# One place for each use: raw weights and row sums in the feed-forward stage of a one-core encoder layer

## The chip, the core and the metric

The kernel runs on one core of a Trainium2 chip. A core has a matrix engine (PE, with its weight loader PEld), a vector engine (DVE), an activation engine (ACT), a general engine (POOL) and a synchronising engine (SP). Each takes its own instructions strictly in the order in which they were queued. Transfers between main memory and the core's own memory are issued from the queue of SP, ACT or POOL, so an issue that has to wait holds up what stands behind it on that engine. All issued transfers share 16 transfer engines.

The metric is the time of one execution in microseconds (us), and the median of several runs is quoted. Beside it stands one profiled execution, from which all rows come.

## What is computed

The reference is one layer of a streaming encoder on 512 tokens of width 1024: four parallel token mixers, a cross-attention, and a gated feed-forward part. The change touches the last of these:

```python
hf = _rms_norm(x, norm_ffn_pre[l])
u = _dwconv_causal(hf @ w_up[l], ffn_dw[l]) + ffn_dw_b[l]
u_g, u_v = jnp.split(u, 2, axis=-1)
yff = (jax.nn.silu(u_g) * u_v) @ w_down[l]
x = x + _rms_norm(yff, norm_ffn_post[l])
```

`w_up` is 1024 x 5632 and `w_down` is 2816 x 1024, so the hidden width of 2816 is 22 blocks of 128 channels. Everything is float32.

## The kernel before

**Products of float32.** Every operand is split in two parts, a rounded high part and the low rest (ACT writes the high part, DVE the low one: L201 and L202 for weights, L1646 and L1647 in the last stage). A product is then three matmuls, all recorded at L244. Split weights go to a ring of four places `wh` and four `wl`; a split must wait until PE has finished with the place four splits earlier.

**The up-projection** (`up_jobs`, L1662) runs over the 22 channel blocks, each with a gate part and a value part. Blocks of even number after the third are done plainly (`plain`, L1691): 8 steps of three 512-column matmuls for each part. Blocks 3, 5, ... 19 are done by `seven` (L1722): the gate and value weights of one block are taken as a 2 x 2 block matrix and multiplied by seven products in place of eight. That needs sums of weights, which POOL makes from the raw weights (L1732 to L1735): it writes the tile `sums` and overwrites parts of the raw tiles `z.g` and `z.v`. One period of the loop at the end of `up_jobs` is one `seven` block and the next plain block. On PE its order is: `a` (body_a, two products), the plain gate part, `b` (two products), the first half of the plain value part, `c`, `d` (one product each), the second half, and `e` (one product). For `b` the split reads `sums`, for `c` the raw tile `z.v`, and for `d` the second half of `z.g`. The next block's `z.g` and `z.v` are loaded on SP's queue (L1740, named `wq`) and `z.g` is split for the next `a`. A weight job is fetched three jobs ahead of its products.

**The sums for the last product.** The down-projection uses seven products too, over 11 pairs of blocks. What it needs of sums of `w_down` is made during the up-projection by `Sums` (L557): for pair q, `load` brings two tiles of 512 KB from `w_down` (L568, named `wp`, on ACT's queue), `add` does four additions of 128 x 512 on POOL (L572 to L575; on DVE for pair 0), and `store` writes both tiles to a buffer in main memory named `sums` (L579, on ACT's queue). The first stored tile is complete after the third addition, the second after the fourth.

**The down-projection** (`down_jobs`, L1827) goes over the 11 pairs twice (phase 0 and phase 1), two jobs for a pair, so 44 raw tiles (`dw`) are loaded on SP's queue from `w_down` and from the stored sums (L591), split by ACT and DVE (L1646, L1647) and multiplied. A job of phase 0 is 12 matmuls of 512 columns. `activations` (L1841) splits the hidden values of a pair; `down_sums` (L1654) has made sums of them on POOL (L1658 to L1660), and a further subtraction on POOL at L1862 prepares phase 1.

**Four places for three uses.** `wp`, `wq` and `dw` tiles, all 128 x 1024, share one tag `dw` with four places. A new tile gets whichever place comes free, and a tile that was named earlier in the program goes first.

**Order.** The order of instructions on each engine is set when the program is built, by a planner that follows the program on a model of the chip: an instruction is queued when the model has its inputs and its place ready. `issue_after(ins)` adds that whatever in the block is on the same engine as `ins` is queued behind it; it puts no condition on instructions of other engines.

Of the kernel before, what the change touches and what calls it, by code (L numbers as in the profile page):

```python
# [17 lines left out]
F32 = mybir.dt.float32  # L18
# [7 lines left out]
P = 128  # L26
# [60 lines left out]
def hybrid_layer(ctx: ExitStack, tc: tile.TileContext, a: dict, out: bass.AP):  # L87
# [1109 lines left out]
    def then(f):  # L1197

        return None, None, f
# [420 lines left out]
    def open_ffn():  # L1620
        bg.drain("n1")
        close(ns.work_)
        close(ns.xp_)
        close(ns.xm_)
        ns.fp_, ns.fp = new_pool("ffn", False)
        ns.work = ns.fp
        ns.quart = [ns.fp.tile([P, 4, S // 2], F32, tag=f"qa{q}", name="qa") for q in range(NF // 2)]
        ns.tok = [ns.fp.tile([P, 4, 4, S // 2], F32R, tag=n, name=n) for n in ("tokh", "tokl")]
        ns.post = ns.fp.tile([P, D], F32, name="g_ffn")
        G.dma_start(ns.post, a["norm_ffn_post"][0].partition_broadcast(P))  # L1630

    def token_sums():

# [28 lines left out]
    def up_jobs():  # L1662
# [19 lines left out]
        def add_sums(q, eng, anchor):  # L1682
            with tc.issue_after(st[anchor]):
                ns.sums.add(q, eng)
# [15 lines left out]
        for n in range(4):  # L1700
            def body(hi, lo, n=n):
                j, i = divmod(n, 2)
                if n == 0:
                    bg.drain("n0")
                ps = bank(("mm", "sc")[n % 2])
                if n == 3:
                    channel_major(ps, (hi, lo), ns.hf, first, lambda: bg.drain("n1"))
                else:
                    (channel_major if n else by_pass)(ps, (hi, lo), ns.hf, first)
                held.append((j, i, ps, (hi, lo)))  # L1710
                if n == 3:
                    open_ffn()
                    ns.sums = Sums(w_down, NF // 2, lambda: ns.fp.tile([P, D], F32, tag="dw", name="wp", bufs=4), A,
                                   "sums")
                    ns.sums.load(0)
                    token_sums()
                    for j, i, ps, w in held:
                        (channel_major if i or j else by_pass)(ps, w, ns.hf, second)
                        done(j, i, ps)
            yield *cols(w_up, n % 2 * DFF + n // 2 * P), body, V, same, HALF_SHIFT  # L1720

        def seven(j):  # L1722

            z = SimpleNamespace()

            def load_a():
                z.g, z.v = [load_block(j, i) for i in range(2)]
                w = split_weights(z.g, [P, NK, P], shift=HALF_SHIFT)
                z.s = ns.fp.tile([P, D], F32, tag="z7", name="sums2")
                a11, a12, a21, a22 = (x[:, c] for x in (z.g, z.v) for c in (slice(0, S), slice(S, D)))  # L1730
                s1, s2 = z.s[:, :S], z.s[:, S:]
                G.tensor_tensor(s1, a21, a22, ALU.add)  # L1732
                G.tensor_tensor(s2, s1, a11, ALU.subtract)
                G.tensor_tensor(a21, a11, a21, ALU.subtract)
                G.tensor_tensor(a12, a12, s2, ALU.subtract)  # L1735
                return w

            def load_block(j, i):
                raw = ns.fp.tile([P, D], F32, tag="dw", name="wq", bufs=4)
                SP.dma_start(raw.rearrange("p (k c) -> p k c", k=NK), block(j, i)[0])  # L1740
                return raw

            def product(ps, w, k0, x, start):
                for k in range(4):
                    mm3(ps, w[0][:, k0 + k], w[1][:, k0 + k], x[0](k), x[1](k), start and k == 0, k == 3, True)

            def part(k0, t):
                return [lambda k, h=h: h[:, k0 + k, (first, second)[t]] for h in ns.hf]

            def summed(i):  # L1750
                return [lambda k, h=h: h[:, i, k] for h in ns.tok]

            def body_a(*w):
                z.r1, z.r2 = bank("sc"), bank("tr")
                z.m = ns.fp.tile([P, 2, HALF], F32, tag="mu", name="mu")
                product(z.r2[:, first], w, 0, part(0, 0), True)
                A.copy(z.m[:, 0], z.r2[:, first])
                product(z.r1[:, first], w, 4, part(4, 0), True)
                V.tensor_tensor(z.r1[:, first], z.r1[:, first], z.m[:, 0], ALU.add)

            def body_b(*w):
                product(z.r2[:, first], w, 4, summed(1), False)
                A.copy(z.m[:, 1], z.r2[:, first])  # L1763
                product(z.r1[:, second], w, 0, summed(0), True)
                A.copy(z.m[:, 0], z.r1[:, second])

            def body_c(*w):
                z.w = w
                product(z.r2[:, first], w, 0, summed(2), False)
                V.tensor_tensor(z.r2[:, second], z.r2[:, first], z.m[:, 0], ALU.add)  # L1770

            def body_d(*w):
                product(z.r1[:, second], w, 0, part(4, 1), False)
                V.tensor_tensor(z.r1[:, second], z.r1[:, second], z.m[:, 1], ALU.add)
                done(j, 0, z.r1)

            def end():
                product(z.r2[:, first], z.w, 4, summed(3), False)
                done(j, 1, z.r2)

            return (load_a, body_a, (lambda: split_weights(z.s, [P, NK, P], shift=HALF_SHIFT), None, body_b),
                    (lambda: split_weights(z.v, [P, NK, P], shift=HALF_SHIFT), None, body_c),
                    (lambda: split_weights(z.g[:, S:], [P, 4, P], shift=HALF_SHIFT), None, body_d), then(end))

        for q, j in enumerate(range(3, NF - 2, 2)):
            load_a, body_a, b, c, d, e = seven(j)
            if q:
                a = load_a, None, body_a
            else:
                a, early = (lambda: (ns,), None, lambda *w: body_first(*early)), []  # L1790
                body_first = body_a
                yield then(lambda f=load_a: early.extend(f()))
                yield plain(2, 0)
                yield plain(2, 1, lambda: (add_sums(0, V, "taps"), sums_step("store", 0, "first")))
            tail = {}

            def first_half(hi, lo, tail=tail):
# [8 lines left out]
                done(j, 1, tail["ps"])  # L1806

            yield a
            yield then(lambda q=q: ns.sums.load(q + 1))
            yield plain(j + 1, 0)  # L1810
            yield b
            yield then(lambda q=q: ns.sums.add(q + 1, G))
            yield (*block(j + 1, 1), first_half)
            if j + 4 > NF:
                ns.pair_sums = []
                yield then(lambda: (down_places(("z7", 2)), down_sums(0, 1)))
            yield c
            yield d
            yield then(lambda q=q: ns.sums.store(q + 1))
            yield then(lambda j=j, f=second_half: f(j + 1))  # L1820
            yield e
        q = NF // 2 - 1
        yield then(lambda: (ns.sums.load(q), down_places(("tokh", 8), ("tokl", 1))))
        yield plain(NF - 1, 0, lambda: (ns.sums.add(q, G), down_sums(2, 3)))
        yield plain(NF - 1, 1, lambda: (ns.sums.store(q), down_sums(*range(4, NF // 2))))

    def down_jobs():  # L1827
        pairs, hold, half = NF // 2, 4, S
# [3 lines left out]
        def load(n):  # L1832
            while len(raws) < min(n, 2 * len(order)):
                (phase, q), job = order[len(raws) // 2], len(raws) % 2
                raw = ns.fp.tile([P, D], F32, tag="dw", name="dw", bufs=4)
                load_parts(raw, ns.sums.parts(phase, job, q))
                raws.append(raw)

# [2 lines left out]
        def activations(phase, q):  # L1841
# [14 lines left out]
            if phase:  # L1856
                split_to(hi, lo, x[:, 1:].rearrange("p a b -> p (a b)"))
            else:
                for i, part in enumerate((x[:, :2], ns.pair_sums[q])):
                    cut = slice(i * S, i * S + S)  # L1860
                    split_to(hi[:, cut], lo[:, cut], part.rearrange("p a b -> p (a b)"))
                G.tensor_tensor(x[:, 1], x[:, 2], x[:, 1], ALU.subtract)  # L1862
            form = dict(a=n, b=256)
            parts[phase, q] = hi.rearrange("p (a b) -> p a b", **form), lo.rearrange("p (a b) -> p a b", **form)

        def weights(phase, q, job):
# [10 lines left out]
                split_to(*both, raw[:, :half])  # L1877
                return [both],
            if (phase, q) == (1, pairs - 1):
                hi, lo = (ns.fp.tile([P, D], F32R, tag="dw", name="dwr", bufs=4) for _ in range(2))  # L1880
            else:
                hi, lo = weights_tile("wh")[:, :D], weights_tile("wl")[:, :D]
            split_to(hi, lo, raw)
# [66 lines left out]
        def ends():  # L1950
# [20 lines left out]
                            next(waiting)  # L1971
                return x

            spare = [ns.fp.tile([P, D], F32, tag="dw", name="o", bufs=4) for _ in range(2)]
            spare.append(gp.tile([P, WB], F32, tag="wr", name="wr", bufs=2)[:, :D])
            with tc.manual_schedule(engines={e.engine for e in (PE, V, A, G)}):
                for name, t, i, x in (("M4", 0, 0, z7), ("M4", 1, 0, z7), ("M2", 0, 0, m1), ("M3", 0, 1, u),
# [78 lines left out]
```

## Time and profile before

| | us |
|---|---|
| median of 3 runs | 1073.95 (1070.86 to 1075.01) |
| the profiled execution | 1072.34 |
| its span, first to last instruction | 1070.5 |
| PE busy in the span | 1034.7 (97%) |
| DVE / ACT / POOL busy | 858.4 / 536.9 / 308.6 |
| stretch 0 to 690 us: PE busy | 687.79 of 690.00 |
| stretch 690 to 945 us (up-projection): PE busy | 237.15 of 255.00 |
| stretch 945 to 1070.5 us (down-projection): PE busy | 109.71 of 125.50 |

Rows of the profile read as follows. A group or timeline row gives the line of the kernel, the engine, the operation, the output tile, an arrow, and the input tiles; in square brackets stands how long the engine was idle before it, and what ended the idle time. A row of waits gives who waited, for whom, the total in us, how often, and the longest. A row of stretches gives the stretch, its length, the busy time of each engine (with the count of instructions), the granted clock of PE, the share of transfer time, and GB/s. The chain of waits is followed back from the last instruction; its rows give the start, the duration and what it was. Matmuls are pipelined and recorded with more than their issue interval, so the interval between starts is PE's true pace.

### The profile page before, as it was taken

To read this page: it belongs to the slowest core of one execution; us is meant where nothing else is said; L and a number is where in the kernel's file an instruction comes from. 1 tells how busy PE (TensorE), PEld (TensorE's weight loads), DVE (VectorE), ACT (ScalarE), POOL (GpSimd) and SP (SyncE) were. 2 spreads that over 40 slices of the span, in tenths; PEclk is the share of its full clock that TensorE was granted. 3 is DMA by queue.
4 is the path that set the end of the run, shared out by engine and by line. 5 is a ranking of instruction groups with operands and counts; after the bars stand their busy time and mean duration, and the time that the engine had idled before them with its cause. 6 is when DMAs were issued, how large, how long until landed. Compare 5 with 4: busy or idle time off the path is not lost.

```text
span 1070.5 us, 15271 instructions
## 1 busy us (share of the span) xinstructions
PE 1034.7 (97%) x5513; PEld 889.1 (83%) x5513; DVE 858.4 (80%) x1283; ACT 536.9 (50%) x898; POOL 308.6 (29%) x319
## 2 busy tenths in 40 slices
PE   9999999999999999999999999998889989997997
PEld 7888888888889988888888999997878879875886
DVE  7899998678787668878679887877766867798796
ACT  5332222386655567657345656544443545544662
POOL 4001000100111144322010310392576555596001
PEclk9999999999999999999999999999989999999999
DMA  7954333334544357756469432344746655526762
GB/s 256 291 169 104 111 99 104 81 99 118 150 115 128 81 143 190 204 159 188 142 217 278 154 119 79 94 130 153 252 143 213 205 189 177 169 87 205 238 205 91
DMA packets 194129, 169.41 MB, mean 158 GB/s; under 512 B 25295, under 2 KB 165692, under 8 KB 194053
## 3 DMA queue, kind: packets, MB, share of 16 engines
q1 hardware_dynamic: 185011, 136.69, 43.0%
q10 hardware_dynamic: 6482, 23.21, 5.9%
q0 software_dynamic: 2560, 8.54, 2.6%
q8 instruction: 43, 0.70, 0.3%
q14 instruction: 33, 0.27, 0.1%
HBM read 142.18 MB, written 26.23 MB: 157 GB/s over the span
## 4 chain that ended last, share of the span: by engine, by line
PE 75%; POOL 12%; DMA 7%; issue 2%; DVE 2%; ACT 1%; ACTq 0%; POOLq 0%; SPq 0%; DVEq 0%
PE ps_mm L244 36%; PE ps_av L244 19%; PE ps_tr L244 10%; PE ps_sc L244 7%; DMA wq<-in_w_up 3%; POOL wp L573 2%; DMA sums<-wp 2%; POOL wp L572 2%; POOL wp L574 2%; DMA wp<-in_w_down 1%; PE ps_tr L250 1%; POOL wq L1735 1%; POOL sums L1732 1%; POOL qa L1660 1%; DVE wl L202 1%
## 5 line engine op out<-in xcount | busy, mean ns | idle before, releaser
L201 ACT CAST wh<-wr 128x1024 fp32r<-128x1024 f32 (+1 forms) x122 | 127.2, 1046 | 174.9 <-PE ps_mm L244 68.9
L202 DVE TENSOR_TENSOR wl<-wr,wh 128x1024 fp32r<-128x1024 f32 (+1 forms) x122 | 162.7, 1336 | 37.1 <-ACT wh L201 36.5
L244 PE MATMUL ps_mm<-hth,wh 128*128 128x512 f32 (+1 forms) x464 | 170.8, 376 | 4.4 <-ACT wh L201 4.0
L244 PE MATMUL ps_mm<-htl,wh 128*128 128x512 f32 (+1 forms) x464 | 170.7, 376 | 0.0
L244 PE MATMUL ps_mm<-hth,wl 128*128 128x512 f32 (+1 forms) x464 | 170.4, 376 | 0.0
L244 PEld LDWEIGHTS ps_mm<-hth,wh 128*128 128x128 f32 x464 | 85.8, 188 | 20.2 <-ACT wh L201 4.2
L244 PEld LDWEIGHTS ps_mm<-hth,wl 128*128 128x128 f32 x464 | 85.7, 188 | 15.5
L244 PEld LDWEIGHTS ps_mm<-htl,wh 128*128 128x128 f32 x464 | 85.6, 188 | 15.0
L244 PE MATMUL ps_av<-htl,wh 128*128 128x512 f32 (+1 forms) x256 | 95.1, 371 | 0.0
L244 PE MATMUL ps_av<-hth,wl 128*128 128x512 f32 (+1 forms) x256 | 95.0, 371 | 0.0
L244 PE MATMUL ps_av<-hth,wh 128*128 128x512 f32 (+1 forms) x256 | 95.0, 371 | 0.0
L697 DVE SCALAR_TENSOR_TENSOR y<-y,par,y 128x508 f32<-128x508 f32 (+29 forms) x120 | 82.8, 730 | 0.1
L244 PEld LDWEIGHTS ps_av<-hth,wl 128*128 128x128 f32 x256 | 48.5, 190 | 8.0
L244 PEld LDWEIGHTS ps_av<-htl,wh 128*128 128x128 f32 x256 | 48.4, 189 | 7.7
L244 PEld LDWEIGHTS ps_av<-hth,wh 128*128 128x128 f32 x256 | 48.5, 189 | 7.5
L1647 DVE TENSOR_TENSOR wl<-dw,wh 128x1024 fp32r<-128x1024 f32 x32 | 43.9, 1373 | 12.9 <-ACT wh L1646 12.8
L202 DVE TENSOR_TENSOR wl<-wq,wh 128x1024 fp32r<-128x1024 f32 (+1 forms) x27 | 34.3, 1270 | 17.2 <-ACT wh L201 14.8
L1646 ACT CAST wh<-dw 128x1024 fp32r<-128x1024 f32 x32 | 33.6, 1050 | 27.1 <-POOL wp L574 8.5
L244 PE MATMUL ps_tr<-hth,wh 128*128 128x512 f32 (+1 forms) x116 | 41.9, 362 | 2.5 <-ACT wh L201 2.5
L244 PE MATMUL ps_tr<-htl,wh 128*128 128x512 f32 (+1 forms) x116 | 41.7, 360 | 0.0
L244 PE MATMUL ps_tr<-hth,wl 128*128 128x512 f32 (+1 forms) x116 | 41.5, 358 | 0.0
L244 PE MATMUL ps_tr<-tokh,wh 128*128 128x256 f32 x108 | 31.6, 292 | 9.5 <-ACT mu L1763 6.1
(555 smaller groups left out, 2810.1 us busy)
## 6 DMA issues: line engine op xcount, KB each, us to landing
wr<-in_w_in SPq DMA_DIRECT2D x38, 512.0 KB
wr<-in_w_gate SPq DMA_DIRECT2D x32, 512.0 KB
wr<-in_w_up SPq DMA_DIRECT2D x26, 512.0 KB
wp<-in_w_down ACTq DMA_DIRECT2D x22, 512.0 KB
sums<-wp ACTq DMA_DIRECT2D x22, 512.0 KB
dw<-sums SPq DMA_DIRECT2D x44, 256.0 KB
wq<-in_w_up SPq DMA_DIRECT2D x18, 512.0 KB
wr<-in_w_branch SPq DMA_DIRECT2D x16, 512.0 KB
```

Of the source, the lines that this page charges most:

```text
L201: last_weights[:] = [order(A.copy(hi, raw[:, :n])).ins, low.tensor_tensor(lo, raw[:, :n], hi.bitcast(F32), ALU.subtract).ins]
L202: low.tensor_tensor(lo, raw[:, :n], hi.bitcast(F32), ALU.subtract).ins]
L244: steps_of[:] = [PE.matmul(ps, lhs, rhs, start=start, stop=stop, skip_group_check=again).ins]
L250: turns.append(PE.transpose(ps, x, ident[:n, :n]).ins)
L572: eng.tensor_tensor(b22, b22, b12, ALU.subtract)
L573: eng.tensor_tensor(b12, b12, b11, ALU.subtract)
L574: eng.tensor_tensor(b11, b22, b11, ALU.add)
L697: ins = V.scalar_tensor_tensor(dst[:, s:], src[:, :S - s], pc("conv_dw", k * 4 + j), dst[:, s:], ALU.mult, ALU.add)
L1646: A.copy(hi, x)
L1647: V.tensor_tensor(lo, x, hi.bitcast(F32), ALU.subtract)
L1660: G.tensor_tensor(x[:, 1], t[:, 0], x[:, 0], ALU.subtract)
L1732: G.tensor_tensor(s1, a21, a22, ALU.add)
```

## The change

- The four places become four tags, `dw0` to `dw3`. A counter for each use walks over its own places: `wp` over `dw0` and `dw1`, `wq` (`z.g`, then `z.v`) over `dw2` and `dw3`, and the `dw` tiles of the last stage over all four in turn.
- In each period the store of pair q, which stood at the end of the period before, is traced after the plain gate part, behind that part's first ACT instruction. The load of pair q+1, which stood behind `a`, is traced after the first half of the plain value part; its anchor is a DVE instruction, while the load is on ACT's queue. The additions of pair q+1 come after `e`.
- At the end, pair 10 is loaded, added and stored after the last plain part, and its additions are DVE's in place of POOL's. The store of pair 9 comes after the last plain gate part.
- In `activations`, the subtraction L1862 of pair q is done when pair q+2 is split (the last three together).

```diff
+    def dw_tile(name, n=4, first=0, dtype=F32):
+
+        i = ns.dw[name] = (ns.dw.get(name, -1) + 1) % n
+        return ns.fp.tile([P, D], dtype, tag=f"dw{first + i}", name=name)
...
-                    ns.sums = Sums(w_down, NF // 2, lambda: ns.fp.tile([P, D], F32, tag="dw", name="wp", bufs=4), A,
-                                   "sums")
+                    ns.sums = Sums(w_down, NF // 2, lambda: dw_tile("wp", 2), A, "sums")
...
-                raw = ns.fp.tile([P, D], F32, tag="dw", name="wq", bufs=4)
+                raw = dw_tile("wq", 2, 2)
...
-                yield plain(2, 1, lambda: (add_sums(0, V, "taps"), sums_step("store", 0, "first")))
+                yield plain(2, 1, lambda: add_sums(0, V, "taps"))
...
             yield a
-            yield then(lambda q=q: ns.sums.load(q + 1))
             yield plain(j + 1, 0)
+            yield then(lambda q=q: sums_step("store", q, "first"))
             yield b
-            yield then(lambda q=q: ns.sums.add(q + 1, G))
             yield (*block(j + 1, 1), first_half)
+            yield then(lambda q=q: sums_step("load", q + 1, "taps"))
...
             yield d
-            yield then(lambda q=q: ns.sums.store(q + 1))
             yield then(lambda j=j, f=second_half: f(j + 1))
             yield e
+            yield then(lambda q=q: ns.sums.add(q + 1, G))
         q = NF // 2 - 1
-        yield then(lambda: (ns.sums.load(q), down_places(("tokh", 8), ("tokl", 1))))
-        yield plain(NF - 1, 0, lambda: (ns.sums.add(q, G), down_sums(2, 3)))
-        yield plain(NF - 1, 1, lambda: (ns.sums.store(q), down_sums(*range(4, NF // 2))))
+        yield then(lambda: down_places(("tokh", 8), ("tokl", 1)))
+        yield plain(NF - 1, 0, lambda: (sums_step("store", q - 1, "taps"), down_sums(2, 3)))
+        yield plain(NF - 1, 1, lambda: (sums_step("load", q, "taps"), ns.sums.add(q), ns.sums.store(q),
+                                        down_sums(*range(4, NF // 2))))
...
-                raw = ns.fp.tile([P, D], F32, tag="dw", name="dw", bufs=4)
+                raw = dw_tile("dw")
...
-                G.tensor_tensor(x[:, 1], x[:, 2], x[:, 1], ALU.subtract)
+                for i in range(max(q - 2, 0), q - 1 if q < pairs - 1 else pairs):
+                    z = ns.quart[i]
+                    G.tensor_tensor(z[:, 1], z[:, 2], z[:, 1], ALU.subtract)
...
-                hi, lo = (ns.fp.tile([P, D], F32R, tag="dw", name="dwr", bufs=4) for _ in range(2))
+                hi, lo = (dw_tile("dw", dtype=F32R) for _ in range(2))
...
-            spare = [ns.fp.tile([P, D], F32, tag="dw", name="o", bufs=4) for _ in range(2)]
+            spare = [dw_tile("dw") for _ in range(2)]
```

More of the change, by code (lines that the diff above doesn't have):

```diff
@@ L1629, in open_ffn @@
         ns.post = ns.fp.tile([P, D], F32, name="g_ffn")
+        ns.dw = {}
         G.dma_start(ns.post, a["norm_ffn_post"][0].partition_broadcast(P))
+    def dw_tile(name, n=4, first=0, dtype=F32):
+        i = ns.dw[name] = (ns.dw.get(name, -1) + 1) % n
+        return ns.fp.tile([P, D], dtype, tag=f"dw{first + i}", name=name)
     def token_sums():
```

## The prediction

> **What bounds the kernel now.** I read the page first, then busy time by stretches, the waits, the chain of waits, and the timelines of single engines. The profiled execution took 1072.34 us, its span 1070.5; the median of the runs is 1073.95, so 1.6 us above. Sums are made against 1072.34, and the difference is carried to the median.
>
> PE is busy for 97% of the span, so only the places where it is not can be won. They lie after 709 us. The stretches below (length, then busy time of PE, PEld, DVE, ACT, POOL, then PE's granted clock) are the up-projection and, after its sum, the start of the down-projection.
>
> ```profile
> span 1070.5 us, 15271 instructions
> 710.00:731.00 21.00, 19.34 (x96) 16.08 (x95) 20.89 (x17) 10.24 (x13) 14.09 (x7) 1.00 0.17 51
> 731.00:753.00 22.00, 18.75 (x107) 16.72 (x108) 16.12 (x23) 9.72 (x14) 7.73 (x5) 0.92 0.71 233
> 775.00:796.00 21.00, 16.75 (x91) 14.74 (x91) 14.79 (x16) 7.32 (x12) 14.04 (x8) 0.88 0.56 180
> 818.00:839.00 21.00, 21.00 (x135) 19.00 (x134) 14.87 (x19) 9.75 (x15) 12.90 (x9) 1.00 0.59 183
> 862.00:885.00 23.00, 18.96 (x106) 16.54 (x106) 14.98 (x17) 8.90 (x13) 13.82 (x10) 0.93 0.50 162
> sum 220.00, PE 202.24 PEld 179.14 DVE 165.86 ACT 99.68 POOL 131.26; mean PE 20.22 PEld 17.91 DVE 16.59 ACT 9.97 POOL 13.13
> 945.00:970.00 25.00, 19.02 (x76) 14.01 (x75) 24.20 (x21) 12.60 (x19) 25.00 (x22) 0.97 0.25 83
> 970.00:1000.00 30.00, 27.08 (x112) 21.30 (x111) 23.30 (x22) 16.99 (x21) 13.21 (x13) 0.97 0.76 254
> ```
>
> In the up-projection PE is idle for 220.00 - 202.24 = 17.8 us. The lowered clock of three stretches is worth at most 0.08 x 22 + 0.12 x 21 + 0.07 x 23 = 5.9 us; part of that falls on the idle time itself, so I take 4: about 21.8 us are lost. In the down-projection it is 5.98 + 2.92 = 8.9 idle and 0.03 x 55 = 1.6 of clock: 10.5. So 32 us are lost in all, and no change to waits here can win more. Some periods lose nothing (818 to 839): the loss is no law of the loop.
>
> What ends the waits:
>
> ```profile
> POOL sums L1732 <- DMA wq<-in_w_up: 57.5, 8, 9.5
> ACT c L1671 <- POOL wp L574: 22.1, 4, 7.5
> SPq L1740 <- DMA sums<-wp: 46.2, 10, 11.0
> 870.47 0.78 ACT L1671 ACTIVATE c<-ps_sc,par 128x512 f32<-128x512 f32 x1 [7.16 <-POOL wp L574]
> 872.23 0.50 PE L244 MATMUL ps_mm<-hth,wh 128*128 128x512 f32 x1 [4.04 <-ACT wh L201]
> ```
>
> ACT issues the store of the sums and must wait for POOL's third addition; the casts that PE needs stand behind that store. At 870 this cost ACT 7.16 us and PE 4.04. And the raw weights `wq` wait on SP for the stored sums to land, since they take the places of `wp`. The chain of waits shows the ring that this makes:
>
> ```profile
> 773.27 1.28 POOL sums L1732
> 779.85 1.26 POOL wp L572
> 785.61 4.40 DMA sums<-wp
> 828.87 2.65 DMA sums<-wp
> 831.60 4.97 DMA wq<-in_w_up
> 836.70 1.51 POOL sums L1732
> 847.61 1.63 POOL wp L574
> 850.63 2.70 DMA sums<-wp
> 853.41 5.65 DMA wq<-in_w_up
> 899.05 6.24 DMA wq<-in_w_up
> 905.42 1.30 POOL sums L1732
> 716.19 5.21 PE ps_av L244 x23
> 721.40 1.42 PE ps_tr L244 x12
> ```
>
> Store 2.65, load 4.97, POOL 12.5 to the end of the third addition (836.70 to 849.24), the fourth addition and the next store: 21.8 us from 828.87 to 850.63. From 773.27 to 905.42 six periods took 22.0 us each. PE's own work in a period is seven products of 12 matmuls (1.42) and two plain parts of 24 (5.21 / 23 x 24 = 5.44): 20.8 us. So ring and PE are almost equal, and every slow POOL addition reaches PE.
>
> **The change, part by part.** *Places bound.* `wp` and `wq` no longer hand places to each other, so the ring is cut: no `wq` waits for a store. *Stores later.* Count from P, the end of a plain gate part. The next `wq` lands at about P + 8.0 (below); POOL's eight operations take 12.5 + 1.3 = 13.8, to P + 21.8. The store is now queued behind the first ACT instruction (0.78) of the next plain gate part, at P + 20.8 + 0.9 = P + 21.7. The third addition is done at P + 20.5, the fourth just then: ACT waits 0 to 1 us, where it waited 7, and I take 0. Its worst is what it was, 7.16. I credit the whole 21.8, less what follows.
>
> *What is late next: the raw weights.* `z.g` now waits on SP for the split for `d`, which reads it last. Its place in the timelines:
>
> ```profile
> 810.60 0.28 PE L244 MATMUL ps_tr<-tokh,wh 128*128 128x256 f32 x1
> 812.93 0.69 DVE L202 TENSOR_TENSOR wl<-wq,wh 128x512 fp32r<-128x512 f32 x1
> 814.30 1.05 ACT L201 CAST wh<-wq 128x1024 fp32r<-128x1024 f32 x1
> 815.38 1.23 DVE L202 TENSOR_TENSOR wl<-wq,wh 128x1024 fp32r<-128x1024 f32 x1 [0.32 <-ACT wh L201]
> 820.38 0.28 PE L244 MATMUL ps_tr<-hth,wh 128*128 128x256 f32 x1
> ```
>
> P is 810.60 (`b` starts). The split for `d` ends at 812.93 + 0.69, P + 3.0; it can't be much earlier, as its place in `wl` is the one that the plain gate part frees. Loading 4.97 brings P + 8.0, cast 1.05 and subtraction 1.23 with 0.3 of hand-over P + 10.6. PE began the next `a` at 820.38, P + 9.8: a wait of 0.8 us in each of eight periods, 6.4 in all. If the planner puts `a` behind the second half and `e`, it is due at P + 12.5 and nothing is lost; with the slowest landing shown, 6.24, it is 2.1 a period, 16.8. I take 6.4, the price of the rows nearest to each other. On SP the two loads of plain weights stand behind `z.g`; they feed parts that come after `a`, so `a` is first to suffer.
>
> By the fit in the Trainium skill, DMA: Bandwidth & Descriptors, section Anatomy of one DMA (a fixed 2.0 us and the bytes at 436 GB/s), a load of 512 KB would take an estimated 3.2 us, there would be no such wait, and the sum would be 6.4 us lower. The rows above with 4.97 to 6.24 us speak against it, and by them I decide.
>
> *Loads of the sums later.* The load waits on ACT's queue for the store of its own tile to land. The only case of that order before:
>
> ```profile
> 754.46 0.78 ACT L1671 ACTIVATE c<-ps_tr,par 128x512 f32<-128x512 f32 x1 [2.89 <-DMA sums<-wp]
> ```
>
> ACT stood still for 2.89 us. Behind the load stand the copies of `b`'s results, which PE needs only after the first half of the next value part, 1.42 + 2.72 = 4.1 us later. So it costs PE nothing, but 1 us in the first period, where DVE is full (20.89 of 21) and the additions of pair 0 are late. Without the cover it would be up to 2.89 a period.
>
> *What stays.* The first two stretches lose 1.66 and 3.25 before any ring turns; I keep 1.66 and 1.3, as part of the second is the wait for POOL. With that 1 us and 0.5 of clock: 4.5. The up-projection keeps 4.5 + 6.4 = 10.9 and wins 10.9.
>
> *The end.* Here a new line for places forms: `dw0` and `dw1` pass from pair 9 to raw tiles 0 and 1, then raw tile 4 and pair 10, and only then raw tile 5.
>
> ```profile
> 883.91 3.35 DMA wp<-in_w_down
> 961.07 7.18 SPq L591 DMA_DIRECT2D dw<-sums  x3
> 964.32 1.04 ACT L1646 CAST wh<-dw 128x1024 fp32r<-128x1024 f32 x1 [2.75 <-DMA dw<-sums]
> L572 DVE TENSOR_TENSOR wp<-wp x1: 680/680/680, 734.1 to 734.1; 128x512 f32<-128x512 f32 x1
> L575 DVE TENSOR_TENSOR wp<-wp x1: 682/682/682, 740.0 to 740.0; 128x512 f32<-128x512 f32 x1
> ```
>
> From P of the last period PE has 12.5 + 2 x 5.44 = 23.4 us of work before the first job of phase 0. Store of pair 8 lands at P + 4.1 (0.9 + two issues + 2.70), load of pair 9 at 8.0 (0.5 + 3.35), three additions 5.8 (779.85 to 785.61) to 13.8, store 2.7 to 16.5, raw tile 0 (0.4 and 964.32 - 961.07 = 3.25) to 20.2, split 2.5 to 22.7. That is 0.7 before it is due; DVE is at 24.20 of 25 there, so I charge 1.5 us of delay. The first job then starts at P + 24.9. Raw tile 4 follows the first split: 24.9 + 3.7 = 28.6, split 31.1; then pair 10: load 3.9, 35.0; four additions on DVE, between 4 x 0.68 = 2.7 and the 6.6 they took for pair 0 (734.1 to 740.7), I take 4, 39.0; store 3.1, 42.1; raw tile 5 3.7, split 2.5: 48.3. Job 5 is due five jobs of 12 x 0.227 = 2.72 after 24.9, at 38.5, or 41.2 if PE takes job 6 first. PE waits 7 us (5.7 to 12 by these ends; 0 if raw tile 5 gets its place before pair 10). With 1.6 of lowered clock behind it, as in the stretch from 862, and 1 for the additions that move to DVE, the end keeps 1.5 + 7 + 1.6 + 1 = 11.1 against 10.5: 0.6 lost.
>
> *L1862 two pairs later* and additions taken off POOL shorten POOL's queue. POOL is full from 945 to 970, but PE waits there for DVE and for raw tiles; I take 0, with 1 us of gain as the other end.
>
> Sum: -10.9 + 0.6 = -10.3, 1062.0 for the profiled execution, 1063.6 for the median; I give 1064.
>
> **The rivals.** *Clean*: `a` is placed late enough, and raw tile 5 does not stand behind pair 10. The up-projection keeps 4.5 (wins 17.3), the end 1.5 + 1 = 2.5 (wins 8.0): 1073.95 - 25.3 = 1048.6. For it speaks 818 to 839 without any loss; against it, that `z.g` cannot be asked for before P + 3.0.
>
> *The wait only changes its name*: raw weights land in 6.24 us, as at 899, and `a` waits 2.1 us eight times. The up-projection keeps 21.3, the end 0.6 more than before: 1074.1, no change. Stores, loads of the sums and raw weights now move together between P + 1 and P + 8, which speaks for it. The Trainium skill, DMA: Bandwidth & Descriptors, section Issuing engines are not separate DMA queues, has transfers of ACT and SP share the same engines; by that rule the landing would be slower as here, and the rows (4.97 beside 6.24) leave it open.
>
> *Slower*: POOL's sums of pairs get ahead of the additions of pair 9.
>
> ```profile
> L1659 POOL TENSOR_TENSOR pairs<-qa 128x256 f32<-128x256 f32 x11 | 13.0, 1182 | 0.0
> L1658 POOL TENSOR_TENSOR pairs<-qa 128x256 f32<-128x256 f32 x11 | 11.3, 1026 | 10.7 <-PE ps_tr L244 7.8 <-DVE wl L202 2.9
> ```
>
> They become ready when `e` is done, at P + 12.5, all at once, and the additions of pair 9 end at 13.8 at the earliest. If in the planner's model the third one comes after that point, it stands behind some 16 operations, 8 x (1.18 + 1.03) = 17.7 us, and raw tile 0 is late by that much: 1063.6 + 17.7 = 1081. In favour: the times are within 1.3 us of each other. Against: the model, not the chip, decides, and the first chance is the additions'.
>
> **How the numbers follow.** The forecast 0.44 (1057 to 1070), clean 0.20, renamed 0.20, slower 0.16. A measurement here tells about 0.5%, 5.4 us, from no change: faster is below 1068.6, slower above 1079.3. Faster: 0.37 of the forecast, 0.20 and 0.05, 0.62. Same: 0.07, 0.14 and 0.02, 0.23. Slower: the rest of the last two, 0.15. The range from 1048 to 1081 reaches to the clean case and to the slower one, whose upper half is left out.
>
> **What would show it.** Right: no row of SP waiting at L1740 for stored sums; ACT waiting for `wp` at L574 below 5 us in all; stretches of PE in the up-projection with under 1.5 us idle; PE waiting near the start of `a` for the split of `wq`; a single wait of 5 to 12 us about 14 us into the down-projection, ended by the split of a raw tile whose SP issue waited for stored sums. Wrong: that wait missing (clean), `a` waiting 2 us a period (renamed), or PE idle for over 10 us before the first job of phase 0 with L1658 between the additions of `wp` (slower).

## The result and the profile after

| | before | after |
|---|---|---|
| median of five runs each, us | 1073.21 (1070.86 to 1075.01) | 1079.37 (1078.18 to 1083.62) |
| after / before, 95% interval | | 1.0066 (1.0039 to 1.0093) |
| profiled execution / its span, us | 1072.34 / 1070.5 | 1078.18 / 1076.4 |

The change makes the kernel slower by 0.7%. Two stages moved, in opposite directions. The timeline of PE shows where: the last product of the up-projection, the first of the down-projection, and the last of all. First the kernel before:

```profile
945.32 0.40 PE L244 MATMUL ps_av<-hth,wl 128*128 128x512 f32 x1
945.55 0.40 PE L244 MATMUL ps_sc<-wh,wr 128*128 128x512 f32 x1
...
1063.09 0.52 PE L244 MATMUL ps_av<-dwr,a 128*128 128x256 f32 x3
```

The changed kernel:

```profile
935.78 0.39 PE L244 MATMUL ps_av<-hth,wl 128*128 128x512 f32 x1
952.60 0.79 PE L244 MATMUL ps_sc<-wh,wr 128*128 128x512 f32 x1 [16.43 <-ACT wh L1652]
...
976.78 1.22 PE L244 MATMUL ps_sc<-wh,htl 128*128 128x512 f32 x2 [5.48 <-ACT wh L1652]
...
984.22 0.62 PE L244 MATMUL ps_mm<-wh,hth 128*128 128x512 f32 x2
...
1068.97 0.52 PE L244 MATMUL ps_av<-dw,a 128*128 128x256 f32 x3
```

The up-projection ends 945.3 - 935.8 = 9.5 us earlier. From there to the last product it was 1063.1 - 945.3 = 117.8 us and is 133.2: 15.4 longer. Together 5.9, the difference of the spans. Two waits, 16.4 and 5.5 us, are new: the first stands where before PE went on at once (945.32, 945.55), and the longest wait of PE in the down-projection before was 3.8 us. The stretches say the same (length, busy time of PE, PEld, DVE, ACT, POOL, then PE's granted clock). Before, the second of them:

```profile
930.00:1000.00 70.00, 61.01 (x262) 48.15 (x263) 61.06 (x57) 36.79 (x50) 47.43 (x42) 0.98 0.46 154
```

The changed kernel:

```profile
710.00:930.00 220.00, 206.11 (x1263) 181.66 (x1262) 176.00 (x191) 101.79 (x148) 141.08 (x79) 1.00 0.54 175
930.00:1000.00 70.00, 48.09 (x194) 38.72 (x193) 51.92 (x50) 30.16 (x40) 42.85 (x41) 0.83 0.51 174
```

PE's idle time from 710 to 930 falls from 17.8 to 13.9 and its clock rises from 0.97 to 1.00; from 930 to 1000 idle time rises from 9.0 to 21.9 and the clock falls from 0.98 to 0.83.

The waits of the changed kernel (who, for whom, total, count, longest; SPq is the queue of transfers on SP):

```profile
PE ps_sc L244 <- ACT wh L1652: 21.9, 2, 16.4
ACT th L1681 <- DMA sums<-wp: 16.9, 6, 3.4
PE ps_tr L244 <- ACT wh L201: 8.7, 7, 1.6
SPq L1745 <- DVE wl L202: 68.3, 16, 6.8
SPq L591 <- POOL wp L575: 10.2, 1, 10.2
SPq L591 <- DMA sums<-wp: 7.9, 2, 5.6
```

In the loop the ring is gone: no row of SP waiting at the load of raw weights (L1745, L1740 before) for stored sums, and none of ACT waiting there for POOL's additions. In its place the raw weights wait for DVE's splits, and PE waits seven times for `a`. ACT's stop for the landing of a store (16.9 in six) is there too, at the place foreseen; no wait of PE is recorded behind it. The last two rows are SP's at the load of raw tiles (L591), and they lead to the two waits of the down-projection.

At the end, POOL's timeline tells the 16.4 us:

```profile
930.08 1.62 POOL L574 TENSOR_TENSOR wp<-wp 128x512 f32<-128x512 f32 x1
931.66 0.73 POOL L1664 TENSOR_TENSOR pairs<-qa 128x256 f32<-128x256 f32 x1
...
944.80 1.71 POOL L575 TENSOR_TENSOR wp<-wp 128x512 f32<-128x512 f32 x1
```

Between the third and the fourth addition of pair 9 stand 13 sums of pairs, from 931.66 to 944.80, 13.1 us. The fourth (L575, `b21 = b21 - b11`) reads the first tile too, so neither `dw0` nor `dw1` comes free before 946.5, though the first tile's store was issued at 931.73. SP stood 10.2 us for it (the row of L575 above), raw tile 0 was issued at 946.54, and the chain of waits follows.

```profile
939.78 1.67 POOL pairs L1665
944.84 1.69 POOL wp L575
946.92 4.56 DMA dw<-sums
```

The 5.5 us belong to raw tile 8, the first of pair 4. In phase 0 the first job of a pair goes to `ps_sc` and `ps_tr` and the second to `ps_mm` and `ps_av`; a first job's raw tile comes half from `w_down` and half from the stored sums, a second job's from the sums alone (in the kernel: `SEVEN` and `parts`). After 952.60 PE's first jobs of pairs 1, 2 and 3 began at 957.42, 965.70 and 968.42, so the first job that waited until 976.78 is that of pair 4. Its place `dw0` went from raw tile 4 to the first tile of pair 10 and then to raw tile 8:

```profile
968.53 0.33 ACTq L579 DMA_DIRECT2D sums<-wp  x1
971.61 0.33 SPq L591 DMA_DIRECT2D dw<-in_w_down  x1
```

The store was issued at 968.53, SP stood 5.6 us until it had landed, and then raw tile 8 was issued. Raw tile 5, behind the other tile of pair 10 on `dw1`, feeds the job at 984.22, which stands behind the first jobs of pairs 4 and 5 in PE's queue, and PE did not wait for it.

### The profile page after: what moved, and what is told of

Read it like the earlier page. It is cut to its first block, busy times and chain, and to the rows that moved or that the text cites. A ratio compares the mean times of both kernels' runs of the same rounds, so it can differ in the third digit from the quotient of the medians.

```text
span 1076.4 us, 15302 instructions
## 1 busy us (share of the span) xinstructions
PE 1029.0 (96%) x5513; PEld 885.0 (82%) x5513; DVE 861.7 (80%) x1287; ACT 533.7 (50%) x898; POOL 317.3 (29%) x315
## 4 chain that ended last, share of the span: by engine, by line
PE 70%; DVE 12%; DMA 8%; issue 4%; ACT 3%; POOL 2%; SPq 0%; ACTq 0%; DVEq 0%; POOLq 0%
PE ps_mm L244 33%; PE ps_av L244 18%; PE ps_tr L244 10%; PE ps_sc L244 6%; DVE wl L202 4%; DMA wq<-in_w_up 4%; DVE c L624 3%; DMA dw<-sums 2%; ACT wh L201 1%; PE ps_tr L250 1%; DVE qa L1683 1%; DMA ptl<-turned 1%; DMA turned<-e 1%; POOL pairs L1664 1%; DVE wl L1653 1%
## 5 line engine op out<-in xcount | busy, mean ns | idle before, releaser
L202 DVE TENSOR_TENSOR wl<-wr,wh 128x1024 fp32r<-128x1024 f32 (+1 forms) x122 | 165.5, 1358 | 33.1 <-ACT wh L201 32.4
L244 PEld LDWEIGHTS ps_mm<-hth,wl 128*128 128x128 f32 x464 | 85.5, 188 | 17.8 <-DVE wl L202 2.3
L244 PEld LDWEIGHTS ps_mm<-hth,wh 128*128 128x128 f32 x464 | 85.6, 188 | 14.8 <-ACT hth L164 0.3
L244 PEld LDWEIGHTS ps_mm<-htl,wh 128*128 128x128 f32 x464 | 85.5, 188 | 14.9
L1681 ACT ACTIVATE th<-c 128x512 f32<-128x512 f32 x22 | 13.9, 632 | 95.0 <-DVE qa L1683 57.0
L202 DVE TENSOR_TENSOR wl<-wq,wh 128x1024 fp32r<-128x1024 f32 (+1 forms) x27 | 37.4, 1385 | 26.2 <-ACT wh L201 26.2
```

Of the source, the lines that this page charges most:

```text
L202: low.tensor_tensor(lo, raw[:, :n], hi.bitcast(F32), ALU.subtract).ins]
L244: steps_of[:] = [PE.matmul(ps, lhs, rhs, start=start, stop=stop, skip_group_check=again).ins]
L1681: A.activation(th, c[:, 0], AF.Silu)
```

## The experiments

All ratios are to the kernel before, on the same chip, with 95% intervals. The last two columns are starts of rows like those above: the last product of the up-projection and the last of all.

| kernel | median, us | ratio | last of up | last of all |
|---|---|---|---|---|
| changed | 1079.37 | 1.0066 (1.0039 to 1.0093) | 935.8 | 1069.0 |
| pair sums behind pair 9 | 1083.56 | 1.0076 (1.0049 to 1.0103) | 939.8 | 1077.7 |
| pair 10 apart | 1071.85 | 0.9964 (0.9943 to 0.9985) | 938.2 | 1063.0 |
| both | 1066.44 | 0.9927 (0.9908 to 0.9946) | 938.2 | 1057.3 |
| raw weights swap | 1075.33 | 1.0003 (0.9987 to 1.0020) | 933.4 | 1066.9 |
| raw tiles start at dw2 | 1081.05 | 1.0064 (1.0043 to 1.0085) | 939.1 | 1072.0 |
| swap, and start at dw2 | 1072.93 | 0.9987 (0.9967 to 1.0007) | 930.7 | 1061.3 |
| behind, apart and swap | 1060.07 | 0.9870 (0.9849 to 0.9891) | 933.8 | 1049.4 |
| order alone | 1060.16 | 0.9863 (0.9823 to 0.9902) | 931.0 | 1050.0 |
| binding alone | 1100.07 | 1.0238 (1.0198 to 1.0278) | 955.7 | 1088.3 |
| L1870 as before | 1079.36 | 1.0047 (1.0030 to 1.0063) | 937.1 | 1072.1 |
| order alone, pair 10 apart | 1056.88 | 0.9844 (0.9820 to 0.9869) | 934.8 | 1048.3 |
| order alone, L1870 as before | 1058.51 | 0.9851 (0.9833 to 0.9870) | 933.3 | 1048.6 |

With the order alone (all three kernels), the binding alone and the start at `dw2` alone, one or two products of the down-projection come before the last of the up-projection, 0.5 us at most. The two columns come from one profiled execution of each kernel, the ratios from all its runs, so small differences between the two say nothing.

**Order and binding apart.** One kernel keeps the new order of steps with the old shared places, the other binds the places in the old order.

```diff
# order alone: the changed kernel, with
-        return ns.fp.tile([P, D], dtype, tag=f"dw{first + i}", name=name)
+        return ns.fp.tile([P, D], dtype, tag="dw", name=name, bufs=4)
# binding alone: the kernel before, with dw_tile(...) of the change at its five places
```

> The changed kernel with the binding alone undone: raw weights, tiles of the sums and raw tiles share four places in turn again; the new order of steps stays. Theory (binding cuts the ring of places): SP waits again at the load of raw weights for stored sums, now stored later in the period, so the up-projection loses more than before, 20 to 45 us against 16 in the changed kernel: 1083 to 1108. Rival (the later store alone frees PE, the binding does nothing in the loop): the up-projection loses 16 as in the changed kernel, and the time is within 3 us of 1079, or less, since the end has four places in turn.

> The kernel before with the binding alone: two places for the sums, two for raw weights, the raw tiles over all four; stores and loads of the sums where they were. Theory (the ring is cut by the binding, the order only takes the wait off ACT): raw weights wait for the split for d and no longer for a store; ACT still waits for POOL's third addition; the up-projection loses between 10 and 21 us, the end keeps its 13 us or gains a wait for pair 10: 1063 to 1075. Rival (binding needs the later store): with two places for the sums the next pair's load waits for the store, POOL's additions fall behind, and it is slower than before: 1075 to 1095.

Both theories fell, and both rivals were right in direction, the second with more than its upper end (1095). The order alone is 1.4% faster than before, the binding alone 2.4% slower. With the order alone, SP's waits at the load of raw weights are all for DVE:

```profile
SPq L1744 <- DVE wl L202: 75.7, 16, 7.1
```

So the ring is cut without the binding: with the store behind the plain gate part and the load behind the first half of the value part, the next raw weights take the places that splits on DVE free. With the binding alone raw weights do not wait for stores either, but the ring closes elsewhere: with two places for the sums, the load of pair q+1 waits for the store of pair q, and POOL for the load.

```profile
POOL wp L572 <- DMA wp<-in_w_down: 46.2, 7, 9.4
PE ps_sc L244 <- ACT wh L1652: 21.1, 1, 21.1
```

The up-projection then ends 10.4 us later than before, and the raw tile of pair 2's first job, which stands behind pair 10, costs 21.1 us more: there pair 10's additions are POOL's, spread between sums of pairs from 967.88 to 985.9.

**What the binding costs at the end.** The first kernel queues the sums of pairs 2 to 10 behind the last addition of pair 9, the second gives pair 10 places of its own, the third does both.

```diff
# pair sums behind pair 9; ns.nine is the last addition of pair 9 (L575)
+    def sums_behind(*pairs):
+        with tc.issue_after(ns.nine):
+            down_sums(*pairs)
...
-                                        down_sums(*range(4, NF // 2))))
+                                        sums_behind(*range(4, NF // 2))))
# pair 10 apart
-                self.held[q] = [self.tile() for _ in range(2)]
+                self.held[q] = [self.tile() if q < self.pairs - 1 else
+                                gp.tile([P, WB], F32, tag="wr", name="wr", bufs=2)[:, :D] for _ in range(2)]
```

> The changed kernel, and the sums of pairs 2 to 10 (L1664, L1665) are put on POOL behind the last addition of pair 9 (L575). Theory: in the changed kernel PE stood for 16.6 us before the first job of phase 0 because the fourth addition of pair 9 was queued behind 13 of these sums (13.1 us), and both places dw0 and dw1 come free only with it. Then that wait falls by about 13 us to some 3, the wait of 5.6 us before job 5 stays, and the median falls from 1079.4 by 11 to 13 to about 1067. Rival: DVE, full in this stretch, or the landing of pair 9's sums holds the first raw tiles back anyway; then the wait stays above 10 and the time within 4 us of 1079. A second rival: the sums of pairs are then late themselves, and the wait moves to jobs 2 to 6: a gain of 0 to 5 us.

> The changed kernel, and the two tiles of the last pair (pair 10) lie in places of their own in place of dw0 and dw1, which the raw tiles of phase 0 use. Theory: the wait of 5.6 us at 971 to 977 is raw tile 5 standing behind pair 10 on dw1; it goes, the wait of 16.6 us stays: 1079.4 - 5 = about 1074.5. Rival: the wait is DVE's, full of splits there, and only 0 to 2 us are won: 1077.5 to 1079.5.

> The changed kernel with pair 10 in places of its own and the sums of pairs 2 to 10 behind the last addition of pair 9. Theory: sums behind took the wait before the first job from 16.6 to 4.5, but lengthened the wait for raw tile 5 from 5.6 to 16.8, as pair 10's additions on DVE stood between splits; with pair 10 apart that wait cannot be, and only the 4.5 and some 3 for late sums stay: 1079.4 - 12 - 5.6 + 3 is about 1065. Rival (the late sums of pairs themselves hold jobs 5 and 6): a wait of 8 to 17 us stays near 968 to 985, 1072 to 1080.

With the sums behind, PE's timeline is:

```profile
943.84 0.74 PE L244 MATMUL ps_sc<-wh,wr 128*128 128x512 f32 x2 [3.67 <-ACT wh L1652]
945.84 1.22 PE L244 MATMUL ps_mm<-wh,wr 128*128 128x512 f32 x2 [0.79 <-ACT wh L1652]
963.42 0.73 PE L244 MATMUL ps_sc<-wh,htl 128*128 128x512 f32 x2 [2.81 <-ACT wh L1652]
...
984.88 1.22 PE L244 MATMUL ps_sc<-wh,htl 128*128 128x512 f32 x2 [16.41 <-ACT wh L1652]
```

The first wait fell from 16.4 to 3.67 + 0.79, as the theory had it, but the one behind pair 10 rose from 5.48 to 16.41 (raw tile 8 again; the expectations name it raw tile 5), another of 2.81 came ahead of it, and nothing was won. DVE's timeline shows part of the reason: pair 10's additions, which had taken 965.07 to 969.22 in the changed kernel, are now parted by the splits of sums that came late.

```profile
965.05 1.22 DVE L572 TENSOR_TENSOR wp<-wp 128x512 f32<-128x512 f32 x1
966.19 1.21 DVE L1653 TENSOR_TENSOR hth<-pairs,hth 128x512 fp32r<-128x512 f32 x1
967.33 1.22 DVE L1653 TENSOR_TENSOR hth<-qa,hth 128x512 fp32r<-128x512 f32 x1
968.47 1.21 DVE L573 TENSOR_TENSOR wp<-wp 128x512 f32<-128x512 f32 x1
...
973.52 1.21 DVE L575 TENSOR_TENSOR wp<-wp 128x512 f32<-128x512 f32 x1
```

The last addition ends at 974.73, 5.5 us later than in the changed kernel. What makes up the rest of the 10.9 us is not taken apart here.

With pair 10 apart the second wait is gone, and of PE's long waits only the first is left:

```profile
955.16 1.22 PE L244 MATMUL ps_sc<-wh,wr 128*128 128x512 f32 x2 [16.56 <-ACT wh L1653]
```

The last product is 6 us earlier than in the changed kernel, near the 5 us expected. The ratio falls by 1.0%, but the intervals allow 0.5%. With both edits the two waits are 6.6 us together, and the ratio is 0.9927:

```profile
PE ps_sc L244 <- ACT wh L1653: 6.6, 2, 3.7
```

So both waits are waits for places, and each edit shows its worth only when the other wait is gone: alone, the sums behind are worth nothing; with pair 10 apart, some 4 us by the ratios (0.9964 to 0.9927, the intervals just touching), and the last product is 5.8 us earlier (1063.0 to 1057.3).

**What the binding costs in the loop.** `z.g` and `z.v` change places each period, so `z.g` takes the one that the split for `c` frees.

```diff
-                raw = dw_tile("wq", 2, 2)
+                n = ns.dw["wq"] = ns.dw.get("wq", -1) + 1
+                raw = ns.fp.tile([P, D], F32, tag=f"dw{(2, 3, 3, 2)[n % 4]}", name="wq")
```

> The changed kernel, and the two tiles of raw weights change places each period: z.g takes the place of the old z.v, which the split for c frees, and z.v the place of the old z.g, which the split for d frees 2 to 4 us later. Theory: the waits of a (1.0 to 1.7 us in seven periods, 10 in all) come from binding z.g to its own place, since the order alone (places shared) showed none of them; they go, the up-projection loses 6 to 10 us in place of 16, and the median falls from 1079.4 to 1070 to 1074. Rival (POOL's sums, which need both tiles, or DVE's full queue set the period): PE waits at the next part instead, and the gain is under 3 us: 1077 to 1080.

The row of PE waiting for the split for `a` (8.7 us) is gone from the waits; the two at the end are 22.1 us together, where they were 21.9:

```profile
PE ps_sc L244 <- ACT wh L1652: 22.1, 2, 12.0
PE ps_sc L244 <- ACT mu L1771: 4.6, 2, 3.0
```

The time falls from 1.0066 to 1.0003, 6.8 us by the ratios, where 5 to 9 were expected. The profiled executions show less: the up-projection ends 2.4 us earlier (933.4) and the last product is 2.0 earlier. PE's idle time from 710 to 930 falls by 5.0, from 13.9 to 8.9, but its granted clock there is 0.98, where it was 1.00. In one period of the changed kernel the second load, `z.g`, was issued at 828.79, behind the split for `d`, and its split began at 834.73; with the swap `z.g` is the first of the two, issued at 820.96, and split at 826.16. Of the 8.7 us 4.6 come back as waits for ACT's copies at L1771 (`mu`, L1770 in the changed kernel), which had no such row.

**Another start for the raw tiles.** The counter of the raw tiles begins at `dw2`, alone and with the swap.

```diff
-        ns.dw = {}
+        ns.dw = {"dw": 1}
```

> The changed kernel, and the raw tiles of the down-projection begin their turn at dw2 (the places of raw weights) in place of dw0: raw tiles 0 and 1 no longer stand behind pair 9, tiles 2 and 3 do, and pair 10 stands ahead of tile 6. Theory: the 16.6 us before the first job are raw tile 0 waiting for pair 9's fourth addition, which POOL does behind 13 sums of pairs; they go, or shrink to 0 to 4 us, since tiles 2 and 3 are due two jobs later, and the wait for pair 10 moves one job on and shrinks from 5.6: 1079.4 - 13 to -20 is 1059 to 1066. Rival (the sums of pairs are then late, or raw tiles 2 and 3 take the wait over): a wait of 8 to 12 us appears at job 2, and the time stays at 1068 to 1076.

> The two edits together: raw weights change places, and raw tiles begin at dw2. Theory (the loss of the changed kernel is in which use is bound to which place, not in binding as such): the gains add, 6 to 9 and 13 to 20 us: 1051 to 1060, as fast as the kernel with shared places (1060.2). Rival (they share a limit, DVE full in both stretches): under 1066 but no better than the raw tiles' edit alone.

Neither theory held, and the times lie above both rivals' ranges too (1081.05 beside 1068 to 1076, 1072.93 beside under 1066): other waits took over, as the first rival has it, though not at the job it names. The wait before the first job goes, and two others take its place (PE's timeline of the kernel with this edit alone):

```profile
950.38 0.77 PE L244 MATMUL ps_av<-wh,wr 128*128 128x512 f32 x1 [6.23 <-DVE c L624]
955.29 1.22 PE L244 MATMUL ps_sc<-wh,hth 128*128 128x512 f32 x2 [3.29 <-ACT wh L1652]
...
981.15 1.22 PE L244 MATMUL ps_sc<-wh,htl 128*128 128x512 f32 x2 [11.90 <-ACT wh L1652]
```

The 11.9 us are a raw tile behind pair 10's first tile again, here raw tile 6 (the first job of pair 3), and the last product is 3 us later than in the changed kernel. Why DVE frees a bank late at 950 stays open. With the swap the kernel is as fast as before; the swap's gain adds, the start's is not there.

**All three mends.** Sums behind pair 9, pair 10 apart, and the swap:

> The changed kernel with all three mends of the binding: raw weights change places, pair 10 lies in places of its own, and the sums of pairs 2 to 10 stand behind pair 9's last addition. Theory (three bindings cost the time, not binding as such): the up-projection loses some 10 us as with changed places alone, the down-projection's start some 12 as with the other two alone: 1066.4 - 5 is 1059 to 1063, the time of shared places (1060.2). Rival (the shared, rotating places are worth something beyond these three): 1065 or more.

The ratio is 0.9870, that of shared places within the intervals (0.9863). The long waits are gone:

```profile
PE ps_sc L244 <- ACT mu L1777: 4.6, 2, 2.4
PE ps_sc L244 <- ACT wh L1653: 2.7, 2, 2.4
```

So three bindings carry the difference between the order alone and the changed kernel, as far as these intervals tell: raw tiles behind pair 9's additions, raw tile 8 behind pair 10, and `z.g` bound to the place that is freed last. Pair 10 apart means two places more (of the tag `wr`), which the order alone does not have; with them it has 0.9844 (below), and that interval overlaps with 0.9870 too.

**The last sums, and the fastest kernel.** L1870 put back to the split of its own pair, in the changed kernel and with the order alone; and the order alone with pair 10 apart.

```diff
-                for i in range(max(q - 2, 0), q - 1 if q < pairs - 1 else pairs):
-                    z = ns.quart[i]
-                    G.tensor_tensor(z[:, 1], z[:, 2], z[:, 1], ALU.subtract)
+                G.tensor_tensor(x[:, 1], x[:, 2], x[:, 1], ALU.subtract)
```

> The changed kernel with the last sums (L1870) where they were: one of them with the split of each pair, in place of two pairs later. Theory (these sums only lengthen or shorten POOL's queue while PE waits for raw tiles): the time is within 3 us of 1079.4. Rival (put off, they take POOL's time from sums of pairs that are due, or free it): at least 4 us faster or slower.

> The kernel with the new order of steps and shared places, and the last sums (L1870) where they were. Theory: the order of stores and loads alone carries the gain of 16 us, and the put-off sums are worth 0 to 2: 1059 to 1063. Rival (they are what lets the down-projection start on time, since POOL is full there): 1065 or more.

> The kernel with the new order of steps and shared places, and pair 10 in places of its own. Theory: with shared places the stretch from 930 to 1000 lost 14 us to splits on DVE and one wait of 3 us for raw tile 5 behind pair 10; that one goes, 1060.2 - 1 to -4 is 1056 to 1059. Rival (DVE is full there, so nothing is won): 1059 to 1062.

Putting the last sums off does nothing that the runs can tell: 1.0047 beside 1.0066 with the binding, 0.9851 beside 0.9863 without, the intervals overlapping in both. The order alone with pair 10 apart has the lowest median, 1056.88, and beats both kernels, by 1.6% (1.3 to 1.8) the one before. Its longest wait of PE at the start of the down-projection is 1.91 us, at 946.61. From the order alone without that edit the intervals do not tell it apart, so the 1 to 4 us expected are not shown.

## Why the prediction was wrong

The forecast was 1064, faster; it came out as 1079.37, slower by 0.7%, near the upper end of the range. By its steps:

- **Up-projection: right in size.** 10.9 us were to be won; its end moved by 9.5. The ring, the wait of ACT and the place of the store were as described. That the size came out is in part luck, for the reason was not as described: "`wp` and `wq` no longer hand places to each other, so the ring is cut" gave the binding the credit, and the runs give it to the order. The binding in the old order lost 10.4 us there.
- **`a` waiting for `z.g`: right in kind, near in size because errors cancel.** 6.4 us in all, at 0.8 a period, became 8.7 at 1.2. The landing had 4.97, and the chain of the changed kernel shows 5.2 to 6.5:

```profile
761.00 6.52 DMA wq<-in_w_up
...
806.76 5.18 DMA wq<-in_w_up
828.79 5.92 DMA wq<-in_w_up
```

  In the period whose `b` starts at 824.07 (P), the load was issued at 828.79, P + 4.7 in place of P + 3.0, and had landed by 834.73, P + 10.7 in place of 8.0. Against that, `a` began at 835.83, as soon as the cast was done, where the prediction had it wait for the subtraction as well, and PE was free at P + 10.2 in place of 9.8: 1.6 us of wait. The swap showed the cause to be the place. The Trainium skill, DMA: Bandwidth & Descriptors, Anatomy of one DMA, by which a load was estimated at 3.2 us, would have had no wait at all. That fit was measured on transfers issued by the general engine, these loads are issued by SP; every row here is longer, and the measurement decides.
- **Load behind the landing of its own store: right.** ACT stood 16.9 us for it, 3.4 at most where 2.89 had been the only row, and PE paid nothing.
- **Raw tile 0: the step that failed.** It was charged 1.5 us and cost 16.4. The sum took POOL's three additions as done at P + 13.8 and went on to the store, "0.7 before it is due". What came true is the third rival: sums of pairs ahead of pair 9's additions, priced at 17.7 and given 0.16. In two details that rival was off as well. It was the fourth addition that was caught, not the third; and that was enough, since L575 reads the first tile, so its place is not free when its sums are complete. The prediction followed the stored data, complete after the third addition, and not the last reader of the place. By the prediction's own figures the fourth addition could begin at P + 13.8 at the earliest, and the sums were ready at P + 12.5, ahead of it; it asked the question of the third alone.
- **A raw tile behind pair 10: right in cause and near in size, wrong in the tile.** 7 us were foreseen, 5.48 measured, and with pair 10 apart the wait is gone. But it is raw tile 8 on `dw0`; the prediction named raw tile 5 and its job, which PE did later and without a wait.
- **L1862 two pairs later: right**, nothing.
- The sum: -9.5 against -10.9, and +15.4 at the end against +0.6. By the prediction's account the end lost 10.5 before, so it now loses about 26: 16.4 before raw tile 0 (1.5 charged), 5.5 behind pair 10 (7 charged), and 4.1 in the two jobs right behind these waits, which took 4.8 and 4.7 us in place of 2.72, at a granted clock of 0.56 and 0.58 (1.6 charged for clock, and 1 for additions on DVE). The miss of 14.8 is the step of raw tile 0, 14.9; the other terms cancel.

What stays open is why the planner put 13 sums between the third and the fourth addition: its model is not in the trace. That their place in POOL's queue, with the places bound, costs the wait is shown by the kernel with both edits (16.56 us with pair 10 apart alone, at most 3.7 with both).

## What to carry to other kernels

A place is free when its last reader is done, not when the result in it is complete; follow that reader's queue before binding a use to a place. Sharing a few places in the order in which they come free can be worth more than giving each use its own: here each of three bindings tied a tile to a place that came free late. Where a change moves steps and binds places together, try each alone: the order was worth 1.4%, the binding cost 2.4% in the old order, and together they cost 0.7%.

## What the runs showed of the hardware

The same DVE instruction took longer while POOL worked. Pair 10's additions in the changed kernel:

```profile
967.39 1.11 DVE L574 TENSOR_TENSOR wp<-wp 128x512 f32<-128x512 f32 x1
968.53 0.69 DVE L575 TENSOR_TENSOR wp<-wp 128x512 f32<-128x512 f32 x1
```

POOL's last instruction beside them ran from 966.77 to 967.95, so the first of the two overlaps it in part and the second does not. With the sums of pairs late, all four took 1.21 or 1.22. Over the changed kernel from 700 us on, DVE's splits of raw tiles (128 x 1024) have a median of 1.67 us where POOL was busy for more than half of the split (7 of them) and 1.23 where it was idle (21), 36% more. So where a sum stands on POOL may also change what DVE's splits cost. The Trainium skill, SBUF — State Buffer, section Who interferes with whom, has a DVE instruction with two inputs from the core's memory contend with a POOL instruction that reads it, by an exclusive lock; the additions and splits here have two such inputs, and the rows agree in sign. No kernel here was made to test this by itself.
